# Down projection of a two-layer encoder: seven block products in place of eight in part of it, with 2048-column weight tiles

## The chip, the core and the metric

One NeuronCore of a Trainium2 chip runs the whole program. The time of a kernel is the device time in microseconds of one execution; for the kernel before it is 1992.83 us, the median of three runs (1992.35 to 1993.45). The engines are named as in the profile: PE is TensorE (PEld its weight loads), DVE is VectorE, ACT is ScalarE, POOL is GpSimd, SP is SyncE, which here issues nearly all DMAs.

## The reference

```python
D_MODEL = 2048; SEQ = 256; DEPTH = 2; D_FF = 5632

def conv_gated_ffn(h, w_up, conv_w, conv_b, w_down):
    a = depthwise_conv_centred(h @ w_up, conv_w, conv_b)
    g, u = jnp.split(a, 2, axis=-1)
    return (jax.nn.silu(g) * u) @ w_down

    for l in range(DEPTH):
        h = rms_norm(x, norm1_g[l])
        q, k, v, gu, gv = jnp.split(h @ w_in[l], splits, axis=-1)
        ... # windowed attention, chunked spatial gating, RMSNorm of both -> mixed
        x = x + mixed @ w_o[l]
        x = x + conv_gated_ffn(rms_norm(x, norm2_g[l]), w_up[l], conv_w[l], conv_b[l], w_down[l])
```

All inputs are float32. The change touches the last product: `y @ w_down`, where y is 256 x 5632 and w_down 5632 x 2048.

## The kernel before

Every large product is computed in float32 quality from three products of fp32r numbers. A weight block comes from HBM into a `raw` tile. ACT rounds it to `hi` (line 128), DVE forms `lo = raw - hi` (line 112, helper `lo_part`), and PE adds hi times activation-hi, hi times activation-lo and lo times activation-hi. The activations are split in the same way into one tile that holds both parts.

`split_weights` loads 128 x 2048 of weights (1 MB) and makes two `hi` and two `lo` tiles of 1024 columns each. The pools hold 3 raw tiles, 4 hi tiles and 4 lo tiles. A tile is taken in turn, and becomes free when its last reader is done.

Each layer runs the input projection, attention and gating, the output projection and then the feed-forward part. That part goes over the 44 column blocks f of 128 of D_FF in two halves, (0, 24) and (24, 44):

- Up projection, `pair`: for two blocks f and f+1 and their two partners, 64 matmuls with hi weights (line 234: 512 columns move, which are the hi and lo activations of 256 tokens) and then 64 with lo weights (line 240, 256 columns). The lo tiles of the second weight of a pair are made late, in `split_later`. The first pair of a layer is `opening`, which takes the weights in smaller steps, since the last activations arrive late. ACT and DVE then sum, convolve, apply SiLU and multiply (`joined`, `convolved`, lines 281 to 283 and 833 to 857), and split the result into an activation tile per f.
- Down projection, `rows_by_cols`: for each of four column groups c of 512 outputs, over the k blocks of the half, four k at a time. Here the activations are the stationary operand and the 512 weight columns move. One load of four k gives 24 matmuls: 4 k, 2 halves m of the tokens (128 each), 3 products (line 168). The two PSUM banks of column group c are added to the residual `xr` by DVE in `residual` (line 614, in the last layer line 883, followed by the output DMA).

PSUM has three double banks (`mmp`) and two single ones (`tpp`). Loads and splits are marked urgent, so that a scheduler puts them ahead of other work on their engine where their buffers allow; the order on each engine is fixed when the program is built. Each engine runs its own list in that order.

## Time and profile before

| quantity | value |
|---|---|
| time of the runs | 1992.83 us (1992.35 to 1993.45), 3 runs |
| profiled execution, span from first to last instruction | 1990.9 us |
| what lies around the span, taken against the median | 1.9 us |
| busy: PE, PEld, DVE, ACT | 1985.5, 1704.8, 1367.6, 1134.5 us |
| HBM read | 378.43 MB, 191 GB/s over the span |

The profile gives the span of the profiled execution and no other time for it, so its own time is set beside the median of the runs. A group is instructions of one line, engine and shape with busy time and mean duration. Consecutive matmuls overlap, so the mean duration of one is longer than its share of time; the pace is read from a run of them in the chain of work that ended last.

### The profile page before, as it was taken

The page shows a single profiled execution, that of the slowest core. Times are in us where ns is not written, and L with a number is a line of the kernel's source. Part 1 is how long each engine was busy: PE and PEld are TensorE (multiplying, and loading weights), DVE is VectorE, ACT ScalarE, POOL GpSimd, SP SyncE. Part 2 cuts the span into 40 slices and gives each one's busy share as a digit, 9 for nine tenths or more (in the row PEclk, how much of TensorE's full clock was granted, in tenths as well). Part 3 has the DMA queues.
Part 4 walks back from the last instruction along what each step waited for, and adds up shares of the span by engine and source line. Part 5 has one row for each costly group of instructions (what it writes and reads, how often), then busy time and mean ns, then how long its engine had stood idle before and what let it go on. Part 6 is the DMA issues. An engine that isn't in the chain of part 4 may idle for free.

```text
span 1990.9 us, 26332 instructions
## 1 busy us (share of the span) xinstructions
PE 1985.5 (100%) x10292; PEld 1704.8 (86%) x10292; DVE 1367.6 (69%) x1930; ACT 1134.5 (57%) x1514; POOL 23.3 (1%) x25
## 2 busy tenths in 40 slices
PE   9999999999999999999999999999999999999999
PEld 8888888888888888888888888888888888888887
DVE  6778677777754577775566786777777445777753
ACT  6786585556543455556667675855555344555542
POOL 0100000000000000000000000000000000000000
PEclk9999999999999999999999999999999999999999
DMA  9754674455555544556767536745545554455563
GB/s 341 243 161 149 219 222 169 170 208 207 198 191 192 188 170 174 212 207 204 219 205 237 161 142 226 198 169 206 207 180 211 191 192 167 171 208 203 201 212 127
DMA packets 95580, 391.15 MB, mean 196 GB/s; under 512 B 43744, under 2 KB 45024, under 8 KB 50912
## 3 DMA queue, kind: packets, MB, share of 16 engines
q1 hardware_dynamic: 94736, 388.74, 56.6%
q8 instruction: 80, 1.31, 0.3%
q10 hardware_dynamic: 720, 0.73, 0.1%
q14 instruction: 44, 0.36, 0.1%
HBM read 378.43 MB, written 2.10 MB: 191 GB/s over the span
## 4 chain that ended last, share of the span: by engine, by line
PE 97%; ACT 1%; DVE 1%; DMA 1%; issue 0%; SPq 0%; POOL 0%; DVEq 0%; ACTq 0%
PE mm L168 42%; PE mm L234 31%; PE mm L240 16%; PE mm L209 2%; PE mm L275 1%; PE tp L168 1%; PE mm L214 1%; PE mm L270 1%; PE tp L308 0%; PE tp L751 0%; PE tp L310 0%; DVE lo L112 0%; PE tp L309 0%; DMA raw<-in_w_up 0%; ACT hi L128 0%
## 5 line engine op out<-in xcount | busy, mean ns | idle before, releaser
L112 DVE TENSOR_TENSOR lo<-raw,hi 128x1024 fp32r<-128x1024 f32 (+1 forms) x708 | 839.4, 1215 | 417.4 <-ACT hi L128 277.1
L128 ACT ACTIVATE hi<-raw 128x1024 fp32r<-128x1024 f32 (+1 forms) x708 | 730.3, 1050 | 606.8 <-PE mm L168 330.9
L168 PE MATMUL mm<-hi,sl 128*128 128x512 f32 x2480 | 667.6, 390 | 0.1
L234 PE MATMUL mm<-sl,hi 128*128 128x512 f32 x2688 | 617.8, 389 | 0.2 <-ACT hi L128 0.2
L234 PEld LDWEIGHTS mm<-sl,hi 128*128 128x128 f32 x2688 | 501.9, 188 | 103.5 <-ACT hi L128 1.1
L168 PEld LDWEIGHTS mm<-hi,sl 128*128 128x128 f32 x2480 | 464.5, 188 | 97.2 <-DVE sl L289 0.9
L168 PE MATMUL mm<-lo,sl 128*128 128x512 f32 x1240 | 382.6, 390 | 0.0
L240 PEld LDWEIGHTS mm<-sl,lo 128*128 128x128 f32 x2688 | 328.1, 192 | 3.3
L240 PE MATMUL mm<-sl,lo 128*128 128x256 f32 x2688 | 329.1, 283 | 0.0
L168 PEld LDWEIGHTS mm<-lo,sl 128*128 128x128 f32 x1240 | 232.5, 188 | 47.9
L838 DVE SCALAR_TENSOR_TENSOR sc<-ev,pc,sc 128x255 f32<-128x255 f32 x176 | 80.6, 481 | 94.0 <-ACT sc L837 94.0
L281 ACT COPY ev<-mm 128x512 f32<-128x512 f32 x96 | 55.4, 577 | 122.5 <-PE mm L240 114.8
L837 ACT ACTIVATE sc<-ev,pc 128x256 f32<-128x256 f32 x176 | 99.1, 589 | 0.0
L841 DVE SCALAR_TENSOR_TENSOR sc<-ev,pc,sc 128x255 f32<-128x255 f32 x176 | 80.6, 481 | 2.9
L296 ACT ACTIVATE sl<-sl 128x256 fp32r<-128x256 f32 x88 | 31.8, 409 | 72.8 <-DVE sl L857 72.8
L283 DVE TENSOR_TENSOR ev<-mm,ev 128x512 f32<-128x512 f32 x96 | 65.6, 683 | 0.0
L209 PE MATMUL mm<-sl,hi 128*128 128x512 f32 x256 | 61.6, 391 | 0.0
L833 DVE TENSOR_TENSOR ev<-ev,rb 128x512 f32<-128x512 f32 x88 | 60.1, 682 | 0.1
L209 PEld LDWEIGHTS mm<-sl,hi 128*128 128x128 f32 x256 | 47.3, 188 | 9.2
L289 DVE SCALAR_TENSOR_TENSOR sl<-sl,pc 128x256 fp32r<-128x256 f32 x96 | 42.6, 479 | 17.7 <-ACT sl L288 17.6
L297 DVE TENSOR_TENSOR sl<-sl 128x256 fp32r<-128x256 f32 x88 | 33.5, 422 | 19.4 <-ACT sl L296 19.4
L288 ACT ACTIVATE sl<-sl,pc 128x256 fp32r<-128x256 f32 x96 | 43.2, 497 | 1.1 <-DMA sl<-in_xT 0.9
(124 smaller groups left out, 813.2 us busy)
## 6 DMA issues: line engine op xcount, KB each, us to landing
raw<-in_w_up SPq DMA_DIRECT2D x172, 1024.0 KB, 5.2
raw<-in_w_down SPq DMA_DIRECT2D x88, 1024.0 KB, 4.9
raw<-in_w_in SPq DMA_DIRECT2D x38, 1024.0 KB, 5.1
raw<-in_w_o SPq DMA_DIRECT2D x32, 1024.0 KB, 4.9
raw<-in_w_gu SPq DMA_DIRECT2D x16, 1024.0 KB, 4.9
raw<-in_w_up SPq DMA_DIRECT2D x8, 512.0 KB, 4.5
sl<-in_prow SPq DMA_DIRECT2D x12, 256.0 KB, 7.3
raw<-in_w_in SPq DMA_DIRECT2D x8, 256.0 KB, 5.2
```

Source lines behind the costliest of these rows:

```text
L112: nc.vector.tensor_tensor(out=lo, in0=part, in1=hi.bitcast(F32), op=ALU.subtract)
L128: nc.scalar.activation(hi[:, cs], part, AF.Copy)
L168: nc.tensor.matmul(ps[m], acts[kk][:, part % 2, m * P : (m + 1) * P], w, start=first and kk == 0 and part == 0, stop=last and kk == KB - 1 ...
L209: nc.tensor.matmul(ps[:, i, :], tile_of(his, k, i), x1, start=k == 0, stop=False)
L234: nc.tensor.matmul(pss[n][:, i, :], hs[k // KB][:, c : c + P], x1, start=k == 0, stop=False)
L240: nc.tensor.matmul(pss[n][:, i, :SEQ], los[k // KB][:, c : c + P], acts[k][:, 0, :], start=False, stop=k == len(acts) - 1)
L281: nc.scalar.copy(rest, ps[:, :, SEQ:])
L283: nc.vector.tensor_tensor(out=s, in0=ps[:, :, :SEQ], in1=rest, op=ALU.add)
L833: nc.vector.tensor_tensor(out=s, in0=s, in1=r2b2[0], op=ALU.mult)
L837: nc.scalar.activation(t[:, i, :], s[:, i, :], AF.Identity, bias=col(3), scale=col(1))
L838: nc.vector.scalar_tensor_tensor(out=t[:, i, 1:], in0=s[:, i, : SEQ - 1], scalar=col(0), in1=t[:, i, 1:], op0=ALU.mult, op1=ALU.add)
L841: nc.vector.scalar_tensor_tensor(out=t[:, i, : SEQ - 1], in0=s[:, i, 1:], scalar=col(2), in1=t[:, i, : SEQ - 1], op0=ALU.mult, op1=ALU.add)
```

## The change

The halves become (0, 22) and (22, 44). In three of the four pairs (half, pair of column groups) of each layer, namely both pairs of the first half and the first pair of the second, three blocks of two k by two column groups are computed with seven products of 128 x 128 by 128 x 512 in place of eight (Winograd's form of Strassen's scheme: the two halves of the tokens, the two k and the two column groups make a 2 x 2 by 2 x 2 block product). This needs:

- sums of activations (`mixed`): DVE makes four combinations of the tiles of y for the three f of `FAST`, ACT and DVE split them;
- sums of weight blocks (`seven`): DVE makes four combinations of the four blocks of a raw tile (three instructions into the new tile `sums`); three of the four blocks themselves are split as before (1536 columns), and all four sums too (2048 columns);
- four more PSUM banks per group, `extra`, and their combination into `xr` at the end of the third block (`seven_out`).

The rest of these pairs is done by `direct`, in blocks of four k as before. The two column groups of a pair now alternate, in the order that `down_blocks` gives. The second pair of the second half has no such blocks, and takes its 22 k as five blocks of four and one of two. The weights of w_down are laid out in HBM in the order of use.

hi and lo tiles are 2048 columns wide, three of each, and each is written by one instruction. The row tiles `q` and `vn` come from the common pool `sl` (48 tiles in place of 43, and no pool `rowp`). The SBUF set aside for dynamic DMA descriptors becomes 1024 bytes per partition.

```diff
+HALVES = ((0, 22), (22, NF))
+FAST = (4, 10, 16)
+def down_blocks(fast, pair, f0, f1):
+    c = (2 * pair, 2 * pair + 1)
+    if not fast:
+        return [((n,), tuple(range(k, min(k + KB, f1))), False) for n in c for k in range(f0, f1, KB)]
+    plain = [k for k in range(f0, f1) if k - f0 - (k - f0) % 2 not in FAST]
+    out = []
+    for i in range(0, len(plain), KB):
+        ks = tuple(plain[i : i + KB])
+        out.append(((c[0],), ks, False))
+        if i // KB < len(FAST):
+            out.append((c, (f0 + FAST[i // KB], f0 + FAST[i // KB] + 1), True))
+        out.append(((c[1],), ks, False))
+    return out
+def is_fast(half, pair):
+    return half == 0 or pair == 0
...
-    slots = pool("slots", 43)
-    rowp = pool("rowp", 4)
+    slots = pool("slots", 48)
-    hip = pool("hip", 4)
-    lop = pool("lop", 4)
+    hip = pool("hip", 3)
+    lop = pool("lop", 3)
+    sump = pool("sump", 1)
...
+            hi = hi_tile()
+            lo = lo_tile() if later is None else None
+            for a in range(0, n, step):
+                cs = slice(a, min(a + step, n))
+                nc.scalar.activation(hi[:, cs], raw[:, cs], AF.Copy)
+                if later is None:
+                    lo_part(lo[:, cs], raw[:, cs], hi[:, cs])
...
+    def mixed(y):
+        t = y.rearrange("p a (m t) -> p (a m) t", t=P)
+        e = sl([P, 4, P])
+        a21 = t[:, 1:2, :].to_broadcast([P, 2, P])
+        nc.vector.tensor_tensor(out=e[:, 0:2, :], in0=a21, in1=t[:, 0:4:3, :], op=ALU.subtract)
+        nc.vector.tensor_tensor(out=e[:, 2, :], in0=t[:, 0, :], in1=e[:, 1, :], op=ALU.subtract)
+        nc.vector.tensor_tensor(out=e[:, 3, :], in0=t[:, 2, :], in1=e[:, 2, :], op=ALU.subtract)
+        return parts(e.rearrange("p a t -> p (a t)"), [P, W])
+
+    def seven(left, right, more, acts, mix, src, used_left, used_right, first, last):
+        with urgent():
+            raw = raw_tile()
+            nc.sync.dma_start(raw, src)
+            hi, lo, his, los = hi_tile(), lo_tile(), hi_tile(), lo_tile()
+            sums = sump.tile([P, 4 * W], F32, tag="sums", name="sums")
+            nc.scalar.activation(hi[:, : 3 * W], raw[:, : 3 * W], AF.Copy)
+            b = raw.rearrange("p (g c) -> p g c", c=W)
+            s = sums.rearrange("p (g c) -> p g c", c=W)
+            b12 = b[:, 3:4, :].to_broadcast([P, 2, W])
+            nc.vector.tensor_tensor(out=s[:, 0:2, :], in0=b12, in1=b[:, 0:3:2, :], op=ALU.add)
+            nc.vector.tensor_tensor(out=s[:, 2, :], in0=s[:, 0, :], in1=b[:, 2, :], op=ALU.add)
+            nc.vector.tensor_tensor(out=s[:, 3, :], in0=s[:, 2, :], in1=b[:, 1, :], op=ALU.add)
+            nc.scalar.activation(his, sums, AF.Copy)
+            lo_part(lo[:, : 3 * W], raw[:, : 3 * W], hi[:, : 3 * W])
+            lo_part(los, sums, his)
...
+        for ps, used, m, a, w, g in (
+            (left, used_left, 0, own(1, 0), (hi, lo), 1),
+            (right, used_right, 0, mix_of(3), (hi, lo), 2),
+            (more, used_more, 0, own(0, 0), (hi, lo), 0),
+            (more, used_more, 1, mix_of(2), (his, los), 2),
+            (more, used_more, 2, mix_of(1), (his, los), 0),
+            (more, used_more, 3, mix_of(0), (his, los), 1),
+            (left, used_left, 1, own(1, 1), (his, los), 3),
+        ):
+            cs = slice(g * W, (g + 1) * W)
...
+            nc.tensor.matmul(ps[m], a[0], w[0][:, cs], start=new, stop=False)
+            nc.tensor.matmul(ps[m], a[1], w[0][:, cs], start=False, stop=False)
+            nc.tensor.matmul(ps[m], a[0], w[1][:, cs], start=False, stop=ps is more and last)
+
+    def seven_out(more, c):
...
+        with urgent():
+            nc.scalar.copy(t, more[0])
+            nc.vector.tensor_tensor(out=v, in0=t, in1=more[1], op=ALU.subtract)
+            nc.vector.tensor_tensor(out=r, in0=more[2], in1=v, op=ALU.subtract)
+            nc.vector.tensor_tensor(out=xr[:, 1, l], in0=xr[:, 1, l], in1=more[3], op=ALU.subtract)
+            nc.vector.tensor_tensor(out=xr[:, 1, h], in0=xr[:, 1, h], in1=more[3], op=ALU.add)
+        nc.vector.tensor_tensor(out=xr[:, 0, l], in0=xr[:, 0, l], in1=t, op=ALU.add)
+        nc.vector.tensor_tensor(out=xr[:, 1, l], in0=xr[:, 1, l], in1=v, op=ALU.add)
+        nc.vector.tensor_tensor(
+            out=xr[:, :, h], in0=xr[:, :, h], in1=r.unsqueeze(1).to_broadcast([P, 2, W]), op=ALU.add
+        )
...
-        for f0, f1 in ((0, 24), (24, NF)):
+        for half, (f0, f1) in enumerate(HALVES):
...
+                if f - f0 in FAST:
+                    mixes[f - f0] = mixed(y)
...
-    nc = bacc.Bacc("TRN2", target_bir_lowering=False, num_devices=1)
+    nc = bacc.Bacc("TRN2", target_bir_lowering=False, num_devices=1, dynamic_dma_scratch_size=1024)
```

Two places show how the order on the engines changes. The first is PE at the start of the down projection of the first half of layer 0. Before, the last lo matmuls of the up projection are followed by blocks of one pattern, four hi and two lo matmuls per k (`mm_5047` holds column group 0, `sl` are the split activations):

```order
L240 MATMUL mm_4846<-sl_2666,lo_4981 128x256 x2
L168 MATMUL mm_5047<-hi_5050,sl_2808 128x512 x4
L168 MATMUL mm_5047<-lo_5051,sl_2808 128x512 x2
L168 MATMUL mm_5047<-hi_5050,sl_2811 128x512 x4
L168 MATMUL mm_5047<-lo_5051,sl_2811 128x512 x2
L168 MATMUL mm_5047<-hi_5054,sl_3011 128x512 x4
L168 MATMUL mm_5047<-lo_5055,sl_3011 128x512 x2
```

Now a block of four k comes first, of which the last k is shown, and then a block of seven products, each of two hi matmuls and one lo matmul (lines 287 to 289). `mm_4520` and `mm_4551` hold column groups 0 and 1, and `mm_4552` and two single banks are `extra`:

```order
L222 MATMUL mm_4520<-hi_4523,sl_2810 128x512 x4
L222 MATMUL mm_4520<-lo_4524,sl_2810 128x512 x2
L287 MATMUL mm_4520<-hi_4557,sl_2997 128x512
L288 MATMUL mm_4520<-hi_4557,sl_2997 128x512
L289 MATMUL mm_4520<-lo_4558,sl_2997 128x512
L287 MATMUL mm_4551<-hi_4557,sl_3004 128x512
L288 MATMUL mm_4551<-hi_4557,sl_3005 128x512
L289 MATMUL mm_4551<-lo_4558,sl_3004 128x512
L287 MATMUL mm_4552<-hi_4557,sl_2994 128x512
L288 MATMUL mm_4552<-hi_4557,sl_2994 128x512
L289 MATMUL mm_4552<-lo_4558,sl_2994 128x512
```

The block of seven products stands between two blocks of four k, and its 21 matmuls take the place of 24.

The second place is DVE a little later in the same stage, where the convolution of the last up pair (lines 838 to 857 before, 958 to 978 now) is still mixed with the splitting of the weights. Before, with two lo tiles per load:

```order
L112 TENSOR_TENSOR lo_5153<-raw_5150,hi_5152 128x1024
L838 SCALAR_TENSOR_TENSOR sc_5033<-ev_5030,pc_92,sc_5033 128x255 x2
L841 SCALAR_TENSOR_TENSOR sc_5033<-ev_5030,pc_92,sc_5033 128x255 x2
L112 TENSOR_TENSOR lo_5157<-raw_5150,hi_5156 128x1024
L857 TENSOR_TENSOR sl_4844<-sl_4844,sc_5033 128x512
L112 TENSOR_TENSOR lo_5187<-raw_5184,hi_5186 128x1024
L297 TENSOR_TENSOR sl_5041<-sl_4844,sl_5041 128x256
L297 TENSOR_TENSOR sl_5044<-sl_4844,sl_5044 128x256
```

Now, from the last weight sum of the second seven-product block (`sums_4656`, whose lo tile is `lo_4655`) to the lo tile of the block of four k after it (`lo_4688`):

```order
L263 TENSOR_TENSOR sums_4656<-sums_4656,raw_4650 128x512
L958 SCALAR_TENSOR_TENSOR sc_4493<-ev_4490,pc_92,sc_4493 128x255
L958 SCALAR_TENSOR_TENSOR sc_4506<-ev_4503,pc_92,sc_4506 128x255
L961 SCALAR_TENSOR_TENSOR sc_4493<-ev_4490,pc_92,sc_4493 128x255
L961 SCALAR_TENSOR_TENSOR sc_4506<-ev_4503,pc_92,sc_4506 128x255
L958 SCALAR_TENSOR_TENSOR sc_4506<-ev_4503,pc_92,sc_4506 128x255
L136 TENSOR_TENSOR lo_4655<-sums_4656,hi_4654 128x2048
L961 SCALAR_TENSOR_TENSOR sc_4506<-ev_4503,pc_92,sc_4506 128x255
L978 TENSOR_TENSOR sl_4333<-sl_4333,sc_4506 128x512
L261 TENSOR_TENSOR sums_4751<-raw_4745 128x1024
L262 TENSOR_TENSOR sums_4751<-sums_4751,raw_4745 128x512
L136 TENSOR_TENSOR lo_4688<-raw_4685,hi_4687 128x2048
```

Five convolution steps have moved ahead of the lo tile of the sums, and two sums of the third block (`sums_4751`) ahead of the lo tile that PE needs earlier. Just ahead of these rows stand, in this order, the lo tile of the block of four k before (2048 columns), the second sum of `sums_4656` and the lo tile of its three plain blocks (1536 columns), and ahead of those the first sum and the lo tile of the block of four k between the first two new ones.

## Prediction

> **What bounds the kernel.** I read the page first: the engine shares, the granted clock, and the chain of work that ended last.

> ```profile
> span 1990.9 us, 26332 instructions
> PE 1985.5 (100%) x10292; PEld 1704.8 (86%) x10292; DVE 1367.6 (69%) x1930; ACT 1134.5 (57%) x1514; POOL 23.3 (1%) x25
> PEclk9999999999999999999999999999999999999999
> PE 97%; ACT 1%; DVE 1%; DMA 1%; issue 0%; SPq 0%; POOL 0%; DVEq 0%; ACTq 0%
> ```

> PE is busy throughout and makes 97% of the chain. A busy PE alone proves little, because matmuls overlap, so I went on to the chain in order of time (start, length, work). The down projection of the first half of layer 0 is the piece at 534.68; the last one is the end of the program.

> ```profile
> 8.84 65.85 PE mm L168 x288
> ...
> 512.48 14.53 PE mm L234 x64
> 527.01 7.67 PE mm L240 x64
> 534.68 130.59 PE mm L168 x576
> ...
> 1960.08 27.21 PE tp L168 x120
> ```

> The pieces join without a hole: 512.48 + 14.53 = 527.01, and so on. The pace of a 512-column matmul is 130.59 / 576 = 0.2267 us here and 27.21 / 120 = 0.2268 us at the end, where twelve matmuls in a row go to one bank. A 256-column one takes 7.67 / 64 = 0.120 us. The program before has 6960 of the first kind, 3168 of the second and 122 small ones (about 0.12 us each by that pace): 1578 + 380 + 15 = 1973 us of the 1990.9. The start (up to 8.84 us, where the first long piece begins) and the tail after the last matmul (3.6 us, rows below) are 12.4 us with few matmuls in them, so all other gaps of PE come to some 6 to 9 us. PE is the bound, and a matmul that goes away is worth its pace as long as the others do not come later. The waits tell who is ahead of whom (who waited for whom, us in total, times, longest):

> ```profile
> ACT hi L128 <- PE mm L168: 330.9, 220, 2.4
> DVE lo L112 <- PE mm L240: 107.7, 40, 3.0
> PEld mm L234 <- ACT hi L128: 1.1, 2, 0.6
> ```

> ACT and DVE wait for PE to give tiles back; PE waits for them 1.1 us in all in the up projection. The question is whether they stay ahead with more work and other tiles.

> **The matmuls removed.** A seven-product block has 21 matmuls where 24 stood. There are 3 blocks in each of 3 groups in each of 2 layers, 18 blocks and 54 matmuls: 54 x 0.2267 = 12.2 us less on the path. All others stay; the new halves only move pairs of the up projection from the first half to the second. In the new blocks three matmuls in a row go to one bank; the 120 matmuls at 1960.08 do so with twelve in a row at the same pace, so I charge nothing. [...]

> **Work added on DVE and ACT.** Durations come from the groups by shape (busy us, mean ns of one):

> ```profile
> L112 DVE TENSOR_TENSOR lo<-raw,hi 128x1024 fp32r<-128x1024 f32 x700 | 834.0, 1221 | 415.2 <-ACT hi L128 275.0 <-PE mm L240 107.7 <-issue 26.2
> L128 ACT ACTIVATE hi<-raw 128x1024 fp32r<-128x1024 f32 x700 | 725.2, 1055 | 604.7 <-PE mm L168 330.9 <-issue 184.8 <-DVE lo L112 18.7
> L841 DVE SCALAR_TENSOR_TENSOR sc<-ev,pc,sc 128x255 f32<-128x255 f32 x176 | 80.6, 481 | 2.9
> L283 DVE TENSOR_TENSOR ev<-mm,ev 128x512 f32<-128x512 f32 x96 | 65.6, 683 | 0.0
> L297 DVE TENSOR_TENSOR sl<-sl 128x256 fp32r<-128x256 f32 x88 | 33.5, 422 | 19.4 <-ACT sl L296 19.4
> L857 DVE TENSOR_TENSOR sl<-sl,sc 128x512 f32<-128x512 f32 x44 | 30.4, 691 | 1.4
> L855 ACT ACTIVATE sl<-sc 128x512 f32<-128x512 f32 x44 | 27.6, 627 | 7.8 <-DVE sc L841 7.5
> ```

> From 512 to 1024 columns DVE needs 1221 - 691 = 530 ns more and ACT 1055 - 627 = 428 ns. Continued, a DVE subtraction of 1536 columns takes 1.75 us and one of 2048 columns 2.28 us; an ACT copy of 2048 columns takes 1.91 us. No row shows these widths; the bounds are one and two instructions of 1024 columns (1.22 and 2.44, 1.06 and 2.11 us). I take the continued values, since both rows lie on the same kind of instruction.

> - A block of four k: DVE 2.28 in place of 2 x 1.22 = 2.44 us, ACT 1.91 in place of 2.11. PE takes 24 x 0.2267 = 5.44.
> - A seven-product block: sums 1.22 + 0.69 + 0.69, lo 1.75 + 2.28, together 6.63 us on DVE; ACT 1.48 + 1.91 = 3.4. PE takes 21 x 0.2267 = 4.76. The sum with a repeated operand has no row; bounds are 0.69 and 1.22 us, and I take the upper one.
> - `seven_out`: six additions or subtractions of 512 at 0.68 to 0.69 and one of 1024 at 1.22, 5.4 us of DVE per group. `mixed`: about 0.42 + 2 x 0.4 + 0.69 = 1.9 us of DVE for each of three f per half, in the up projection.

> A group with new blocks is 8 blocks of four k and 3 new ones: PE 8 x 5.44 + 3 x 4.76 = 57.8 us. DVE has 8 x 2.28 + 3 x 6.63 + 5.4 + 4 x 0.69 (residual) = 46.3 us. In the first group of a half there is also the rest of the last convolution, 8 x 0.48 + 3 x 0.69 + 2 x 0.42 = 6.8 us, 53.1 us in all. Such counting meets the trace before: 24 loads x 2.44 + 8 x 0.69 + 6.8 = 70.9, and the stage shows 70.31 (the columns are window, length, DVE busy and its instructions, PE clock, DMA share, GB/s):

> ```profile
> 534.70:665.30 130.60, 70.31 (x70) 1.00 0.60 207
> ```

> So DVE goes from half busy to 80% and 92% of these groups and stays under PE. All of it is beside matmuls, as long as the work is early enough. The price if it is not stands with the rivals.

> **The tightest place.** Time 0 is the start of the down projection of a half; P is a block of four k, S a new one. PE: P0 0 to 5.4, S1 to 10.2, P1 to 15.6, P2 to 21.1, S2 to 25.8, P3 from 25.8. With three hi and three lo tiles of 2048 (a new block takes two of each) P1 reuses the tile of P0, free at 5.4; ACT is done at 7.4 and DVE at 9.7. Then DVE runs the rows shown with the change: sum 10.9, lo of P2 13.2, sum 13.9, lo of S2 15.6, sum 16.3, five convolution steps 18.7, lo of the sums of S2 21.0, convolution step and product 22.2, two sums of S3 24.1, lo of P3 26.4. PE needs this lo after its first four matmuls, at 25.8 + 0.9 = 26.7. The margin is 0.3 us by mean durations. In a run of instructions DVE is faster than their means, as the timeline of DVE at the end of the up projection shows (start, length):

> ```profile
> 513.21 0.69 DVE L283 TENSOR_TENSOR ev<-mm,ev 128x512 f32<-128x512 f32 x1
> 513.82 0.68 DVE L833 TENSOR_TENSOR ev<-ev,rb 128x512 f32<-128x512 f32 x1
> 514.41 2.35 DVE L112 TENSOR_TENSOR lo<-raw,hi 128x1024 fp32r<-128x1024 f32 x2
> 528.00 4.63 DVE L112 TENSOR_TENSOR lo<-raw,hi 128x1024 fp32r<-128x1024 f32 x4 [3.01 <-PE mm L240]
> ```

> Starts lie 0.60 us apart for 0.69 us instructions, and four of 1.22 us take 4.63. Some 8% off the 16.7 us from 9.7 to 26.4 make the margin about 1.6 us. The load that the sums of S3 need can start when S2's raw tile is free, at 16.3, and is wanted at 22.2. The DMA rows (count, KB, median us to landing), and one slow load in the chain:

> ```profile
> raw<-in_w_up SPq DMA_DIRECT2D x172, 1024.0 KB, 5.2
> raw<-in_w_down SPq DMA_DIRECT2D x88, 1024.0 KB, 4.9
> ```

> ```profile
> 1716.96 1.23 DVE lo L112
> 1718.24 6.90 DMA raw<-in_w_up
> 1725.24 1.07 ACT hi L128
> 1726.35 11.19 PE mm L234 x48
> ```

> At 4.9 it lands at 21.2, at 6.9 at 23.2, 1.0 us late, which the margin of 1.6 absorbs. I charge 0 here; the upper bound, by means and with the slow load, is 1.0 - 0.3 = 0.7 us in each of the four halves, 2.8 us. The second group of a half has no convolution and has 6.8 us more room. The last four rows also show today's tight spot of the up projection: the lo tiles of the second weight wait for PE, their raw tile is free late, and the load just makes it. With three full lo tiles the first of the two late tiles no longer waits for this pair's matmuls, so this place gets looser: a gain of at most the gaps there, some 0.4 us.

> **Wider tiles elsewhere.** The first matmul of a block now waits for a copy of 1.91 us in place of 1.06. In the steady stages three tiles of 2048 hold half as much again as four of 1024, and cover it. Where activations arrive late it can cost. The opening of layer 0 needs its last activations (start, length; ACT, DVE, then PE):

> ```profile
> 282.18 1.05 ACT L128 ACTIVATE hi<-raw 128x1024 fp32r<-128x1024 f32 x1
> 284.40 0.87 DVE L289 SCALAR_TENSOR_TENSOR sl<-sl,pc 128x256 fp32r<-128x256 f32 x2
> 284.44 2.00 PE L275 MATMUL mm<-sl,hi 128*128 128x512 f32 x8
> ```

> DVE ends at 285.27 and the fifth matmul of that row is due at 284.44 + 4 x 0.227 = 285.35, so there is no slack. In the new order a weight copy of 1.91 us stands ahead of the residual copies (0.9 later than now), while the copy of 1.05 us at 282.18 stands behind. I take 0; if both are late it costs 0.9 + 0.9 us in each layer, 3.6 in both. In the attention stages the order is laid out anew with the wider tiles. Their gaps are part of the 6 to 9 us above; I take 0.5 us more, with bounds of -1 and +3.

> **SP, pools, tail.** SP issues 90 loads of w_down in place of 88 with the same bytes. The pool `sl` holds at its fullest 16 + 22 + 6 (mixed) + 2 tiles of 48. The smaller descriptor space has no row of its own; I take 0. The end of the program:

> ```profile
> 1984.60 0.69 DVE L883 TENSOR_TENSOR xr<-tp,xr 128x512 f32<-128x512 f32 x1 [6.30 <-PE tp L168]
> 1986.89 0.39 PE L168 MATMUL tp<-lo,sl 128*128 128x512 f32 x1
> 1987.32 0.76 DVE L883 TENSOR_TENSOR xr<-tp,xr 128x256 f32<-128x256 f32 x2 [2.03 <-PE tp L168]
> 1988.11 0.35 ACTq L884 DMA_DIRECT2D out_x<-xr  x1
> ```

> The last block now has two k, so the first addition starts 1.36 us before the end of PE in place of 2.7. It ends 0.7 us before it all the same; its output DMA then overlaps the last ones, 0 to 0.5 us, taken as 0.2.

> **Sum.** -12.2 + 0.5 + 0.2 = -11.5 us: the span goes from 1990.9 to 1979.4, and with the 1.9 us around it (median 1992.83 less the span) the time is 1981.3 us. A measurement of this kernel tells a change of about 0.2% (4 us) from none.

> **Rivals.**

> (a) DVE becomes the bound, and the kernel is slower. A new block costs DVE 6.63 us against 4.76 of PE. If the list of DVE could not run ahead, because the lo of the sums waits for a tile and everything behind it waits too, each new block would stall PE by up to 1.87 us: 18 x 1.87 = 33.7, time 1992.8 - 12.2 + 33.7 = 2014. It decides from 12.2 / 18 = 0.68 us per block. For it: the 107.7 us of waits of DVE for PE, so its list does stop at such a tile. Against it: the walk above, in which each block is ready before PE needs it. [...] Chance 0.06.

> (b) The wide tiles delay openings and attention, and the tight place stalls: all upper bounds, 3.6 + 3 + 2.8 + 0.5 = 9.9, a time of 1992.8 - 12.2 + 9.9 = 1990.5; about half of it is likelier, 1985.6. For it: no slack at 285.27. Against it: ACT is 57% busy. Chance 0.20, of which a quarter ends within 0.2% of the time before.

> (c) The deeper buffers also remove gaps: up to 2 us of those 6 to 9, time 1979. Chance 0.10.

> (d) The change doesn't save its matmuls' time, because the pace in the new blocks is slower: from 54 x 0.2267 / 378 = 32 ns more on each of their 378 matmuls the gain is gone, time 1992.8. The even pace of both pieces of the chain speaks against it. Chance 0.03.

> (e) As summed, 1981.3, from 1980 to 1983: 0.61.

> **Range and chances.** From (c) through (e) to the middle of (b): 1979.2 to 1986.0, which leaves out 0.06 + 0.03 + 0.10. Slower: (a), less the part of it that a small stall leaves near zero, 0.04. Same: 0.02 of (a), 0.03 of (d), 0.05 of (b), less a little for what may still gain, 0.07. Faster: 0.89.

> **What would show it.** Right: 6906 matmuls of 512 columns; the stage of the first half of the down projection is one piece of the chain on PE, 2 x 57.8 = 115.6 us long, with DVE about 100 us busy; 21 matmuls in 4.76 us; PE's waits for hi and lo still near 1 us. Wrong: PE waiting for the lo of line 136 or the sums' hi of line 264 at every new block (a), gaps before the opening or in attention (b), or a pace above 0.227 us at lines 287 to 289 (d).

## Result, and the profile after

The changed kernel takes 1982.22 us (median of five runs, 1982.12 to 1982.53) against 1992.86 us before (five runs, 1992.35 to 1993.45). The ratio is 0.9948 with a 95% interval of 0.9936 to 0.9959: 10.6 us faster. The forecast was 1981.3 us in a range of 1979.2 to 1986.0, faster with a chance of 0.89.

The page of the changed kernel has the same shape as before: PE is busy for 1973.7 of 1980.7 us at a granted clock of 1.00 and carries 97% of the chain, and only DVE's share has grown, from 69% to 73%.

```profile
span 1980.7 us, 25342 instructions
PE 1973.7 (100%) x10238; PEld 1694.4 (86%) x10238; DVE 1444.5 (73%) x1744; ACT 1116.2 (56%) x1199; POOL 19.5 (1%) x25
PEclk9999999999999999999999999999999999999999
PE 97%; DVE 1%; DMA 1%; ACT 1%; issue 0%; SPq 0%; POOL 0%; DVEq 0%; ACTq 0%
```

PE has 54 instructions less (10292 to 10238), and the span 10.2 us less (1990.9 to 1980.7). Where they went is read off the chain in order of time, cut at the first up projection of each layer (`x64` pieces), at the start of the next layer and at the last piece. Before (start, length, work):

```profile
74.91 27.67 PE mm L168 x122
...
290.41 14.53 PE mm L234 x64
...
887.31 176.82 PE mm L168 x780
...
1280.72 14.53 PE mm L234 x64
```

In the third row 480 matmuls belong to the second half of the down projection (20 k, 4 column groups, 6 each), so layer 0 ends at 887.31 + 480 x 0.2267 = 996.14. The last piece of before, shown in the prediction, ends at 1987.29. After:

```profile
76.55 33.56 PE mm L195 x148
...
292.87 14.53 PE mm L354 x64
...
992.48 59.40 PE mm L195 x262
...
1277.50 14.53 PE mm L354 x64
...
1947.18 29.93 PE tp L222 x132
```

| stretch | before, us | after, us | difference |
|---|---|---|---|
| program's start, its first 300 projection matmuls | 74.91 | 76.55 | +1.64 |
| rest of layer 0 up to its first up projection | 215.50 | 216.32 | +0.82 |
| feed-forward of layer 0 | 705.73 | 699.61 | -6.12 |
| layer 1 up to its first up projection | 284.58 | 285.02 | +0.44 |
| feed-forward of layer 1 | 706.57 | 699.61 | -6.96 |
| after the last matmul | 3.61 | 3.59 | 0 |
| span | 1990.9 | 1980.7 | -10.2 |

The two feed-forwards are now equal to 0.01 us. In each, 27 matmuls went, and 27 x 0.2267 is 6.12: in layer 0 this gain came out to the last hundredth, and layer 1 gained 0.84 us more, for which the first experiment below gives the place.

The start of the first down projection, in the chain and in a window (length, then busy us of PE, PEld, DVE, ACT, POOL, the clock, DMA share, GB/s):

```profile
514.94 5.47 PE mm L222 x24
520.40 0.23 PE mm L287
...
525.16 10.88 PE mm L222 x48
```

```profile
514.94:630.57 115.63, 115.63 (x511) 95.76 (x511) 93.26 (x78) 54.49 (x38) 0.00 (x0) 1.00 0.59 213
```

A new block fills 520.40 to 525.16, 4.76 us for 21 matmuls, and the two groups take 115.63 us without a hole; 115.6 was forecast. DVE is busy for 93.3 us of it. At the tightest place (P3, which begins after the second new block) DVE and then PE read:

```profile
537.82 2.29 DVE L136 TENSOR_TENSOR lo<-raw,hi 128x2048 fp32r<-128x2048 f32 x1
541.55 0.61 PE L222 MATMUL mm<-lo,sl 128*128 128x512 f32 x2
```

The lo tile is ready at 537.82 + 2.29 = 540.11, and the first matmul that reads it starts at 541.55. The margin is 1.44 us.

The one wait that is new and long stands at the start of the program, where PE waits for the first lo tile that is split in one piece of 2048 columns (chain, then the timeline of PE):

```profile
15.41 1.93 ACT hi L158
17.36 2.30 DVE lo L136
19.71 56.62 PE mm L195 x248
```

```profile
17.39 1.20 PE L195 MATMUL mm<-hi,sl 128*128 128x512 f32 x4
19.71 0.74 PE L195 MATMUL mm<-lo,sl 128*128 128x512 f32 x2 [1.13 <-DVE lo L136]
```

The four hi matmuls would be done at 17.39 + 0.91 = 18.30, and the next one starts at 19.71: 1.41 us of nothing. Before, ACT could start on this raw tile 0.3 us earlier, and its first half needed one ACT copy and one DVE subtraction of 1024 columns (1.06 and 1.22 us by the means) in place of 1.93 and 2.30:

```profile
15.11 1.06 ACT L128 ACTIVATE hi<-raw 128x1024 fp32r<-128x1024 f32 x1 [1.76 <-DMA raw<-in_w_in]
```

### The profile page after: what moved, and what is told of

Read it like the earlier page. It is cut to its first block, busy times and chain, and to the rows that moved or that the text cites. A ratio compares the mean times of both kernels' runs of the same rounds, so it can differ in the third digit from the quotient of the medians.

```text
span 1980.7 us, 25342 instructions
## 1 busy us (share of the span) xinstructions
PE 1973.7 (100%) x10238; PEld 1694.4 (86%) x10238; DVE 1444.5 (73%) x1744; ACT 1116.2 (56%) x1199; POOL 19.5 (1%) x25
## 4 chain that ended last, share of the span: by engine, by line
PE 97%; DVE 1%; DMA 1%; ACT 1%; issue 0%; SPq 0%; POOL 0%; DVEq 0%; ACTq 0%
PE mm L354 31%; PE mm L195 19%; PE mm L222 18%; PE mm L360 16%; PE mm L328 2%; PE tp L222 2%; PE mm L395 1%; PE mm L333 1%; PE mm L287 1%; PE mm L288 1%; PE mm L289 1%; PE mm L390 1%; DVE lo L136 1%; DMA raw<-in_w_in 1%; PE tp L428 0%; PE tp L287 0%
## 5 line engine op out<-in xcount | busy, mean ns | idle before, releaser
L136 DVE TENSOR_TENSOR lo<-raw,hi 128x2048 fp32r<-128x2048 f32 (+1 forms) x360 | 792.7, 2214 | 368.5 <-PE mm L360 185.7
L158 ACT ACTIVATE hi<-raw 128x2048 fp32r<-128x2048 f32 (+1 forms) x342 | 640.9, 1874 | 372.2 <-PE mm L195 121.1
L354 PEld LDWEIGHTS mm<-sl,hi 128*128 128x128 f32 x2688 | 502.1, 188 | 102.5
L195 PE MATMUL mm<-hi,sl 128*128 128x512 f32 x1152 | 312.8, 391 | 0.0
L222 PE MATMUL mm<-hi,sl 128*128 128x512 f32 x1032 | 275.9, 389 | 0.0
L195 PEld LDWEIGHTS mm<-hi,sl 128*128 128x128 f32 x1152 | 215.2, 188 | 45.3 <-ACT hi L158 0.8
L222 PEld LDWEIGHTS mm<-hi,sl 128*128 128x128 f32 x1032 | 193.5, 188 | 39.9
L195 PE MATMUL mm<-lo,sl 128*128 128x512 f32 x576 | 179.0, 391 | 1.1 <-DVE lo L136 1.1
L222 PE MATMUL mm<-lo,sl 128*128 128x512 f32 x516 | 158.8, 389 | 0.0
L195 PEld LDWEIGHTS mm<-lo,sl 128*128 128x128 f32 x576 | 107.8, 188 | 24.2 <-DVE lo L136 2.0
L222 PEld LDWEIGHTS mm<-lo,sl 128*128 128x128 f32 x516 | 96.9, 188 | 20.1
L958 DVE SCALAR_TENSOR_TENSOR sc<-ev,pc,sc 128x255 f32<-128x255 f32 x176 | 77.6, 478 | 9.2 <-ACT sc L957 8.9
L961 DVE SCALAR_TENSOR_TENSOR sc<-ev,pc,sc 128x255 f32<-128x255 f32 x176 | 77.4, 478 | 0.3
L403 DVE TENSOR_TENSOR ev<-mm,ev 128x512 f32<-128x512 f32 x96 | 65.6, 684 | 0.3 <-ACT ev L401 0.3
L264 ACT ACTIVATE hi<-sums 128x2048 fp32r<-128x2048 f32 x18 | 34.5, 1918 | 53.8 <-PE mm L222 53.8
L136 DVE TENSOR_TENSOR lo<-sums,hi 128x2048 fp32r<-128x2048 f32 x18 | 41.2, 2290 | 25.9 <-ACT hi L264 25.5
## 6 DMA issues: line engine op xcount, KB each, us to landing
raw<-in_w_up SPq DMA_DIRECT2D x172, 1024.0 KB, 5.1
raw<-in_w_down SPq DMA_DIRECT2D x86, 1024.0 KB, 4.9
raw<-in_w_in SPq DMA_DIRECT2D x38, 1024.0 KB, 5.0
raw<-in_w_o SPq DMA_DIRECT2D x32, 1024.0 KB, 4.8
raw<-in_w_gu SPq DMA_DIRECT2D x16, 1024.0 KB, 5.0
```

Source lines behind the costliest of these rows:

```text
L136: nc.vector.tensor_tensor(out=lo, in0=part, in1=hi.bitcast(F32), op=ALU.subtract)
L158: nc.scalar.activation(hi[:, cs], raw[:, cs], AF.Copy)
L195: nc.tensor.matmul(ps[m], acts[kk][:, part % 2, m * P : (m + 1) * P], w, start=first and kk == 0 and part == 0, stop=last and kk == KB - 1 ...
L222: nc.tensor.matmul(ps[m], acts[kk][:, part % 2, m * P : (m + 1) * P], w, start=first, stop=done and kk == len(acts) - 1 and part == 2,)
L354: nc.tensor.matmul(pss[n][:, i, :], hs[k // UB][:, c : c + P], x1, start=k == 0, stop=False)
L403: nc.vector.tensor_tensor(out=s, in0=ps[:, :, :SEQ], in1=rest, op=ALU.add)
```

## Experiments

Two theories stood against each other. Theory 1: PE sets the time, the gain is the count of matmuls, and it is kept only because the new blocks stand apart, so that DVE is ahead of PE by a small margin at each. The rival: the count of matmuls isn't what matters (the wide tiles are), or DVE has room everywhere and the spacing means nothing. Each run has its own runs of the kernel before on the same chip: 1993.23 us for the first four, 1992.61 for the next four, 1992.74 for the last two.

**The wide tiles without the seven blocks**, with the pools and halves of the changed kernel.

```diff
 def is_fast(half, pair):
-    return half == 0 or pair == 0
+    return False
...
-                if f - f0 in FAST:
+                if f - f0 in FAST and is_fast(half, 0):
```

> The changed kernel with no seven-product block: all four pairs of column groups in blocks of four k, no mixed activations, but with the 2048-column tiles, the pools and the halves of the changed kernel. Theory 1 (the 54 matmuls are the whole gain, and the wide tiles cost about 1.6 us at the start and in attention): 1982.2 + 12.2 = 1994.4 us, 1.6 above the kernel before; the stages of the feed-forward part last exactly as long as their matmuls. Rival 2 (the new blocks cost something hidden that eats part of the 12.2): less than 1994.4, down to the 1992.9 of before. Rival 3 (the wide tiles bring a gain of their own and the seven products less than 12.2): below 1992.9.

Measured: 1994.48 us, ratio 1.0006 (0.9997 to 1.0014), span 1992.4 us. Its chain, cut at the same places:

```profile
76.28 33.56 PE mm L195 x148
...
292.55 14.53 PE mm L354 x64
...
998.27 59.40 PE mm L195 x262
...
1283.08 14.53 PE mm L354 x64
...
1958.88 29.93 PE tp L222 x132
```

The feed-forwards take 705.72 and 705.73 us. So the seven blocks are worth 6.11 and 6.12 us in the two layers, and nothing else in them moved. What the wide tiles, with their pools and halves, do by themselves is here too: the start is 1.37 us later than before, the rest of layer 0 up to its up projection 0.77 longer, layer 1 up to there 0.23 longer, and the feed-forward of layer 1 0.84 shorter. That last is what two late weight tiles cost before, where PE starts late at 1681.44 and 1726.35 us and the hi matmuls of the two pairs take 14.86 and 15.05 us in place of 14.53; the prediction had named this place.

**The first wide lo tile in four steps.** Only the two loads of the second k block in the input projection of layer 0 are split in steps of 512 columns.

```diff
-    def rows_by_cols(ps, acts, src, first, last, raw=None, apart=False):
+    def rows_by_cols(ps, acts, src, first, last, raw=None, apart=False, step=4 * W):
-        hi, lo = split_weights(src, raw, None, 4 * W if raw is None else W)
+        hi, lo = split_weights(src, raw, None, step if raw is None else W)
...
-            rows_by_cols(ps, acts[b * KB : b * KB + KB], src, b == 0, b == NB - 1, raw)
+            rows_by_cols(ps, acts[b * KB : b * KB + KB], src, b == 0, b == NB - 1, raw, False, W if l == 0 and b == 1 else 4 * W)
```

> The changed kernel, except that the two loads of the second k block in layer 0's input projection are split in four steps of 512 columns in place of one of 2048. In the trace of the changed kernel PE waits there at 17.39 us for a lo tile of 2048 columns. Theory 1 (the start lost about 1.5 us to the width of this one instruction): 1980.7 us, and the gap at 17.4 is gone or under 0.3 us. Rival 2 (the load lands late, and width has no part): 1982.2 us.

Measured: 1981.18 us (1980.79 to 1981.83), ratio 0.994 (0.9928 to 0.9953). The gap at 17.4 us is gone, and the layer's first up projection starts at 290.93 in place of 292.87. Of these 1.94 us, 0.58 are given back in layer 1 ahead of its up projection (285.60 in place of 285.02). The wide tile at the start was the cost, though the run has steps of 512 columns and not the 1024 of before; the stage with attention of layer 1 differs by up to a microsecond from kernel to kernel (284.58 us before, 284.81 with the wide tiles alone, 285.02 in the changed kernel, 285.60 here).

**The three new blocks of a group in a row.**

```diff
-        if i // KB < len(FAST):
-            out.append((c, (f0 + FAST[i // KB], f0 + FAST[i // KB] + 1), True))
+        if i == KB:
+            out += [(c, (f0 + f, f0 + f + 1), True) for f in FAST]
```

> The changed kernel with the three seven-product blocks of a group directly after one another (in the middle of the group) in place of one between every two to three blocks of four k. Same instructions. Theory 1 (a new block needs 6.6 us of VectorE against 4.76 of TensorE and is covered only by the blocks of four k beside it, as far as three tiles and one tile of sums let VectorE run ahead): a stall of 2 to 4 us in each of 6 groups, 1994 to 2006 us, as slow as before or slower. Rival 2 (VectorE's share over a whole group, 80 to 92%, is what counts): 1982 us, no change.

Measured: 2000.1 us (1999.59 to 2001.06), ratio 1.0035 (1.0022 to 1.0048): 17.9 us slower than the changed kernel with the same matmuls. The waits of PE, and the chain at one of the six stalls:

```profile
PE mm L287 <- ACT hi L264: 11.4, 6, 2.4
```

```profile
599.34 1.76 DVE lo L136
601.10 1.15 DVE sums L261
...
602.27 0.70 DVE sums L262
...
603.00 0.70 DVE sums L263
...
603.81 1.92 ACT hi L264
...
605.77 0.50 PE mm L287
```

Between two blocks lie 1.15 + 0.70 + 0.70 us of sums on DVE and 1.92 of their split on ACT, one behind the other. The row at 599.34 is the lo tile of the block's plain part, which stands on DVE's list between the lo tile of the sums of the block before (597.06 to 599.35) and the new sums; whether the one tile or the order of the list holds the sums back, the run with two tiles below decides. PE waits for the hi tile of the sums (line 264). Theory 1 had the size. But the waits make only 11.4 us of what was lost: in the profiled execution the two feed-forwards are 10.2 and 8.7 us longer than in the changed kernel, 18.9 in all. Much of the rest is what follows the waits, in PE's timeline:

```profile
542.35 0.39 PE L289 MATMUL mm<-lo,sl 128*128 128x512 f32 x1
545.06 0.64 PE L287 MATMUL mm<-hi,sl 128*128 128x512 f32 x1 [2.32 <-ACT hi L264]
545.50 0.63 PE L288 MATMUL mm<-hi,sl 128*128 128x512 f32 x1
...
549.27 0.40 PE L289 MATMUL mm<-lo,sl 128*128 128x512 f32 x1
```

A window shows the clock there (length, busy us of PE, clock, DMA share, GB/s):

```profile
545.27:548.68 3.41, 3.41 (x9) 0.50 0.52 219
```

Before the wait, matmuls start 0.23 us apart; after it 0.43, with a granted clock of 0.50. From 545.06 to 549.27 eleven matmuls start, which costs 4.21 - 11 x 0.2267 = 1.7 us more than their pace. Three such stretches come to 4.8 us; 1.0 us is the start of PE after the six waits (the gaps are 12.4 us long), and of the 18.9 us 1.7 stay unassigned.

**More work on DVE, at each new block.** The subtraction that makes the lo tile of the sums is done twice, 18 x 2.29 = 41 us more for DVE.

```diff
             lo_part(los, sums, his)
+            lo_part(los, sums, his)
```

> The changed kernel with the lo tile of the weight sums computed twice in each of the 18 new blocks: 2.29 us more of VectorE per block, 6.9 per group, same result. Theory 1 (VectorE is beside the matmuls, with 1.4 us to spare at the tightest place, the block of four k after the second new block in the first group of a half, and more than 6 us in a second group): stalls of 2 to 5 us in the first group of each of four halves, none in the two second groups: 1990 to 2000 us. Rival 2 (there is room everywhere, as the busy shares of 75 to 87% say): 1982.2 to 1984 us. Rival 3 (VectorE bounds each new block already): 18 x 2.29 = 41 us more, 2023 us.

Measured: 1983.56 us (1983.22 to 1985.39), ratio 0.9954 (0.9941 to 0.9968), 1.3 us above the changed kernel. The same two groups of the first half, which run here from 516.78 to 632.41, and then the first of them alone:

```profile
516.78:632.41 115.63, 115.63 (x511) 95.73 (x511) 105.75 (x84) 54.75 (x38) 0.00 (x0) 1.00 0.58 213
516.78:574.50 57.72, 57.72 (x256) 47.76 (x256) 56.45 (x50) 28.09 (x23) 0.00 (x0) 1.00 0.62 225
```

DVE is busy for 105.8 of 115.63 us, in the first group for 56.45 of 57.72, and PE hasn't lost a tenth of a microsecond there; the feed-forwards take 699.61 and 699.62 us. Here the rival was right, and theory 1's 1990 to 2000 us wrong. The margin of 1.44 us is not a margin on work. Nor does this run repeat the list that was walked: the first two sums of the third block now stand (from 544.01 us) behind the lo tile that PE needs first (from 539.60), so the order of the list moved with the work. In the run with three in a row the two groups have less DVE work than here (93.6 us), and PE waits. So that stall must be something else than the amount of DVE work. The profiled execution of this run is the slowest of its four (1985.39 us); its start is taken up in the last section.

**Without the sums.** The three instructions that make the sums are left out, and the raw tile is used in their place, so the products are not the reference's.

```diff
-            nc.vector.tensor_tensor(out=s[:, 0:2, :], in0=b12, in1=b[:, 0:3:2, :], op=ALU.add)
-            nc.vector.tensor_tensor(out=s[:, 2, :], in0=s[:, 0, :], in1=b[:, 2, :], op=ALU.add)
-            nc.vector.tensor_tensor(out=s[:, 3, :], in0=s[:, 2, :], in1=b[:, 1, :], op=ALU.add)
+            sums = raw
```

> The changed kernel without the three weight sums on VectorE: the four plain blocks are split in their place, so the products are not those of the reference. 2.6 us less of VectorE in each of 18 blocks, and ScalarE need not wait for them. Theory 1 (TensorE bounds these stages, all work on the sums lies beside matmuls): 1982.2 us, within 0.5. Rival 2 (part of the missing 1 us of gain is lost at the new blocks): 1981 or less.

Measured: 1982.45 us (1982.07 to 1983.17), ratio 0.9949 (0.9936 to 0.9961). The feed-forwards take 699.60 and 699.62 us: the sums cost PE nothing there.

**Three in a row, with two tiles for the sums.** The order of the run with three in a row (2000.1 us), with a second `sums` tile; to make room, three row tiles and one scratch tile less.

```diff
-    slots = pool("slots", 48)
+    slots = pool("slots", 45)
-    sump = pool("sump", 1)
-    scr = pool("scr", 4)
+    sump = pool("sump", 2)
+    scr = pool("scr", 3)
```

> The kernel with the three new blocks in a row (2000.1 us), with two sums tiles in place of one; to make room, 45 tiles in the common pool and 3 convolution tiles. Theory 1 (the stall comes from the chain through the one sums tile: sums 2.6 us, their hi tile 1.9, their lo tile 2.3, and only then the sums of the next block, 6.8 us for a block that TensorE does in 4.76): with two tiles the chains of two blocks overlap and most of the 18 us goes, 1983 to 1990 us. Rival 2 (VectorE's work of 6.6 us per block is the limit, with whatever tiles): 1996 to 2000 us.

Measured: 1982.34 us (1982.01 to 1982.54), ratio 0.9947 (0.9932 to 0.9963). All six waits for line 264 are gone, and the time is below the 1983 to 1990 us that were expected. The 17.9 us were the chain through one buffer: the sums of a block can be written only when the lo of the block before has read the tile, and then their split must follow. The spacing of the blocks in the changed kernel hides this chain; a second tile hides it as well.

**Four new blocks in each group.** A fourth takes the place of a plain block of two k; 18 matmuls fewer.

```diff
-FAST = (4, 10, 16)
+FAST = (4, 8, 12, 16)
...
-        out.append(((c[0],), ks, False))
-        if i // KB < len(FAST):
-            out.append((c, (f0 + FAST[i // KB], f0 + FAST[i // KB] + 1), True))
+        at = (c, (f0 + FAST[i // KB], f0 + FAST[i // KB] + 1), True)
+        out += [((c[0],), ks, False), at] if i < 3 * KB else [at, ((c[0],), ks, False)]
```

> The changed kernel with four seven-product blocks in each of the three groups of a layer in place of three (at k offsets 4, 8, 12, 16; the fourth stands ahead of the last two blocks, which have two k each). 18 matmuls fewer. Theory 1 (TensorE still bounds the groups: 57.1 us of matmuls against some 55 us of VectorE in a first group): 1982.2 - 18 x 0.2267 = 1978.1 us. Rival 2 (the first groups of a half are full on VectorE, so the fourth block gives back in stalls what it saves): 1981 to 1984 us.

Measured: 1978.6 us (1978.34 to 1979.17), ratio 0.993 (0.9917 to 0.9942). 18 x 0.2267 = 4.1 us were to be had, and 3.6 came: each feed-forward is 1.9 us shorter (697.73 and 697.70), and the start, in the profiled execution, 0.4 longer.

**The same, with the fine start, and also in the last pair of column groups of layer 0** (12 more matmuls fewer).

```diff
-def is_fast(half, pair):
-    return half == 0 or pair == 0
+def is_fast(half, pair, l):
+    return half == 0 or pair == 0 or l == 0
...
```

The layout of w_down in HBM follows this order, now layer by layer.

> A version meant to beat both kernels: four seven-product blocks per group, also in the second pair of the second half of layer 0 (28 blocks in place of 18, 30 matmuls fewer), and the finer split of the two early loads. Theory 1: 1982.2 - 30 x 0.2267 - 1.0 = 1974.4 us. Rival 2 (the groups have no room for a fourth block): 1979 to 1982 us.

Measured: 1980.34 us (1979.78 to 1983.84), ratio 0.9941 (0.9929 to 0.9954): slower than the run with fewer new blocks. The figure is the rival's (1979 to 1982, no room for a fourth block), but its reason isn't, since a fourth block gained in the run before. Everything up to about 912 us gains; the chain at the change of layers shows the loss:

```profile
986.47 6.38 DMA raw<-in_w_in
...
995.84 4.38 DMA sl<-sl
...
1007.35 6.05 DMA sl<-sl
...
1017.04 34.37 PE mm L194 x150
```

In the changed kernel the chain holds only PE there. Now the input projection of layer 1 waits: the gaps of PE between 979 and 1017 us come to 4.3 us, and two in the last pair to 1.7. In place of a whole column group at a time, the last two groups finish close together, and with them the additions into `xr` that the next layer's activations wait for. That this is what delays them is read from the chain; no run tests it by itself.

**The two gains that hold, together, and the input projection in finer steps.** First four new blocks and the fine start (the diffs of both runs above), then also all other loads of the input projection in two steps of 1024 columns:

```diff
-            rows_by_cols(ps, acts[b * KB : b * KB + KB], src, b == 0, b == NB - 1, raw, False, W if l == 0 and b == 1 else 4 * W)
+            rows_by_cols(ps, acts[b * KB : b * KB + KB], src, b == 0, b == NB - 1, raw, False, W if l == 0 and b == 1 else 2 * W)
```

> Four pairs of seven blocks in each half (as in the run with four), and the second load of the program split in four steps of 512 columns. If the wait at 17.4 us for a 2048-wide lo tile is one cost and the six matmuls of a fourth pair another, independent of it, both gains add: 1978.6 - 1.0 = 1977.6 us, PE's wait of 1.41 us at 17.9 gone, ratio near 0.9925. It also parts the run with four pairs in every column group (1980.3) in two: if that one lost through its start, this one loses too and ends above 1979; if it lost at the layer's end through the second pair of column groups, this one stays at 1977 to 1978.

> The same, and all other loads of the input projection split in two steps of 1024 columns, as before the change (one more ScalarE and one more VectorE instruction for each load). If the 0.4 to 0.7 us that attention lost is the width of these tiles, it comes back: 1977.0 us, with the next layer's stage ahead of its feed-forward at 284.6 us instead of 285.0. If it is the order in which the scheduler now puts the rest, or only scatter of DMA times, it stays within 0.3 of the run without this (1977.6). If the added instructions weigh, up to 0.5 above it.

Measured: 1976.59 us (1976.2 to 1978.57), ratio 0.9921 (0.9907 to 0.9934), for the first, and 1977.42 us (1976.95 to 1977.84), ratio 0.9922 (0.991 to 0.9935), for the second. The first, in the chain:

```profile
74.57 39.00 PE mm L194 x172
...
290.89 14.53 PE mm L353 x64
...
988.59 59.40 PE mm L194 x262
...
1273.49 14.53 PE mm L353 x64
```

Both gains add, with 1.0 us more than their sum (0.7 when each run is taken against its own runs of the kernel before): the start is at 74.57, even earlier than before's 74.91, and the feed-forward takes 697.70 us. It is the fastest version, 16.2 us below before and 5.6 below the changed kernel. Since it shares its start with the run that had new blocks everywhere, that run lost at the end of layer 0, not at its start. The finer steps elsewhere bring none of the gain they were tried for, and the time is 0.8 us above the run without them: layer 0 reaches its up projection 0.77 us earlier (290.12), and layer 1 takes 1.13 longer for the same stretch (286.03 in place of 284.90). So the 0.4 to 0.8 us that attention takes more in the changed kernel is not shown to be the width of the tiles; the order that the scheduler lays out there, and the scatter of the DMAs (2.9 to 10.1 us from issue to landing for loads into `raw` in the changed kernel, 5.0 in the median), remain open as causes.

## Why the prediction was right, step by step

- **The matmuls removed**: right in size and place. 12.2 us were forecast; the feed-forwards with and without the seven blocks differ by 6.11 and 6.12. The pace in the new blocks is the old one (4.76 us for 21), so rival (d) is out.
- **Work added on DVE and ACT**: the continued durations held, as the groups by shape show (busy, mean ns):

```profile
L136 DVE TENSOR_TENSOR lo<-raw,hi 128x2048 fp32r<-128x2048 f32 x330 | 751.5, 2288 | 359.7 <-PE mm L360 185.7 <-ACT hi L158 166.4 <-PE mm L333 5.2
L158 ACT ACTIVATE hi<-raw 128x2048 fp32r<-128x2048 f32 x330 | 631.7, 1914 | 360.0 <-PE mm L195 121.1 <-PE mm L222 104.6 <-DMA raw<-in_w_up 28.3
L136 DVE TENSOR_TENSOR lo<-raw,hi 128x1536 fp32r<-128x1536 f32 x18 | 31.5, 1751 | 0.0
```

  2.28, 1.75 and 1.91 us had been worked out for them from two rows each. The sum with a repeated operand took 1.22 us in each of 18 cases, the upper bound. DVE was busy for 93.3 us of the two groups, where 46.3 + 53.1 = 99.4 had been added up: in a run of instructions one starts before the record of the last ends (2.20 us apart for 2.29, in the timeline), which the sum of durations doesn't see.
- **The tightest place**: 1.44 us of margin where 1.6 had been walked out, and no wait; the charge of 0 was right. The reason was only half right, though. Rival (a), a list of DVE that can't run ahead, comes true in another order of the blocks, where it costs 17.9 us, and its cause is the one tile of the sums, not the 6.63 us of DVE work per block against 4.76 of PE: 41 us more of such work cost 1.3, none of it in the feed-forwards. The prediction had priced the throughput and left this chain out. Its price, 1.87 us at each of 18 blocks = 33.7 us, was too high: even in that order each group stalls only once, at the third of its three blocks.
- **The gain of a looser up projection**, at most 0.4 us and not in the sum, was 0.84: both gaps of before went, in the run without the seven blocks too. This is rival (c) in small. The room that (c) was given, 6 to 9 us of gaps in PE, came from a slip: the page's 10292 matmuls leave 164 small ones and not 122, and with the numbers as they stand 1990.9 - 1973 - 12.4 is 5.5 us. The sum doesn't use it.
- **Wider tiles elsewhere**: the step that missed. It asked about openings and attention and not about the first loads of the program, where nothing is ahead of anything; the start cost 1.64 us, of which PE's wait for the wide tile makes 1.41. The cause, one wide instruction in place of narrower ones on a path from a DMA to PE, is the one that the step gives for the opening. The opening of layer 0 cost nothing, as taken; attention took 0.82 + 0.44 = 1.26 us more where 0.5 was taken, inside its bounds.
- **SP, pools, tail**: 0.2 forecast, 0 measured (3.61 and 3.59 us).

The span was to fall by 11.5 us and fell by 10.2. The 1.3 us between are +1.6 (start), +0.8 (attention), -0.8 (up projection) and -0.2 (tail). Misses of 2.4 us to one side and 1.0 to the other partly cancelled, which is luck; the main term was exact.

## What to carry to other kernels

Where PE sets the time without holes, count the matmuls that go and multiply by their pace (27 x 0.2267 = 6.12 us per layer here, and 6.11 and 6.12 came); then search for the few places where nothing is ahead of anything (the program's start, the change of layers), because that is where wider tiles and other orders cost here (1.64 us at the start of the changed kernel, 4.3 us of gaps at the change of layers with new blocks in the last pair too), and split only those loads finely (the two early ones: 1.0 us gained; then all of the input projection: 0.8 lost). For an engine that is beside the bound, its total load said little here (41 us more on DVE cost 1.3): follow the longest chain through a tile that exists once (DVE, ACT, DVE through `sums`, which cost 17.9 us), and either space its users or give it a second buffer. In this kernel the scheme with fewer products paid at every place where it was tried except the last one before a dependent stage; there look at what the next stage waits for before two column groups are made to finish together.

## What was not expected of the hardware

Some waits of PE cost more than their length. In the run with three new blocks in a row, three of the four waits of about 2.5 us were followed by 3 to 4 us in which matmuls of 512 columns started 0.43 us apart in place of 0.23; the fourth, and the two of 1.2 us, were not. Each slow stretch added 1.5 to 1.7 us.

The length of the wait alone did not decide. The 1.41 us wait at the start of the changed kernel was not followed by a slower pace: 248 matmuls behind it take 56.62 us, 0.228 us each. In the profile of the run with more work on DVE the same wait of 1.41 us, which there follows another of 0.5 us with four matmuls between, was: the 248 matmuls take 58.11 us. The granted clock tells more. In each of the four slow stretches it is 0.50 for 3.41 us, and the three of the run with new blocks in a row start at 545.27, 910.49 and 1903.77 us, 107 and 291 times 3.413 us apart. The windows below (columns as above) are cut by this grid: first the one before the first slow stretch, then the two across which the fourth wait of 2.5 us falls (1537.35 to 1539.87); the last two rows are of the run with more work on DVE.

```profile
541.85:545.26 3.41, 1.09 (x5) 1.00 0.36 86
...
1535.12:1538.53 3.41, 2.39 (x11) 1.00 0.00 0
1538.53:1541.94 3.41, 2.07 (x9) 1.00 0.87 303
```

```profile
17.10:20.52 3.42, 1.78 (x7) 1.00 0.99 411
20.52:23.93 3.41, 3.41 (x10) 0.50 1.06 404
```
